# An empty step ahead of a head's first value products, and the last product of a convolution copied out of its PSUM bank

## The chip, the core and the metric

The kernel runs on one core of a Trainium2 chip. The core has TensorE (matrix products, PE in the profile, its weight loads PEld), VectorE (DVE), ScalarE (ACT), GpSimd (POOL) and SyncE (SP, here a queue that issues transfers). They run side by side and wait for each other through semaphores. Products are written into PSUM, eight banks of 128 x 512 floats, and are read out of it by VectorE and ScalarE; everything else lies in SBUF. The metric is the device time of one execution in microseconds (us), as the median of the runs.

## The reference, cut to what matters

Two layers of one mixer, over 1024 positions and 1024 columns, with eight heads of 256 in each layer: four mLSTM heads, whose q and k go through a short causal convolution and a SiLU, and four retention heads, whose q and k are rotated.

```python
for l in range(DEPTH):
    h = rmsnorm(x, norm_g[l]) * (1.0 + scale) + shift
    p = h @ w_in[l]
    mq, mk, mv, mo, mz, mi, mf, rq, rk, rv, rz = split_cols(p)
    qk = jax.nn.silu(causal_dwconv(jnp.concatenate([mq, mk], -1), conv_w[l], conv_b[l]))
    cell = mlstm_chunkwise(...)        # four heads
    y_m = sigmoid(mo) * head_layernorm(cell, gn_m[l]) * silu(mz)
    ret = retention_chunkwise(...)     # four heads
    y_r = head_layernorm(ret, gn_r[l]) * silu(rz)
    x = x + gate * (jnp.concatenate([y_m, y_r], -1) @ w_out[l])
return rmsnorm(x, final_g)
# within a head, for each chunk of positions:
#   s = (q k^T) * decay;  o = s v + (q C) * decay;  C = decay * C + k^T v
```

## The kernel before

**Products.** Every operand is split into a high part and a rest, and each product is three matmuls (`mm3`, lines 181 to 183). The projections of a layer run as a list of jobs. A job takes two blocks of 128 columns (q, k, or a gate) and builds them out of seven products of 12 matmuls, in the manner of Strassen: a11, S1, S2, a12, S4, S3, a22. A job for values (`v`) takes two heads, and each of its seven products comes in two parts of 24 smaller matmuls. One such product or part is called a slot here; there are 238 of them in a layer. The weights of a slot are loaded by SP some seven slots ahead, their high part is made by ScalarE (L408) and the rest by VectorE (L413).

**Banks.** The products of a q or k job gather in three banks: one called X, used by a11, S2, S3 and a22, one called Y and one called Z. Y and Z share a pair of buffers (`pz`), X has a pair of its own (`px`), which the jobs take in turn. A value job takes both buffers of each pair: its third slot (a11, part 0) starts in one `px` buffer and its fourth (a11, part 1) in the other, which the job ahead of it used for its own X.

**Convolution.** `pair_product` hands each finished quarter to `done`. For q and k of the mLSTM heads that launches `conv_chain`: one scaled copy by ScalarE (L889), three shifted multiply-adds by VectorE (L894), a tanh (L897) and a last multiply (L899). For the quarter of the last product, a22, the chain reads its input straight from the X bank, so the bank is free when the third multiply-add has read it. Before that, `halo` (L767) copies the last three columns of the bank.

**Attention of a head.** It runs between the slots. After each slot the kernel ticks, and the head whose turn it is does the next step of `TABLE` (L985). A step is a list of short words. `S0` to `S3` are the scores of a chunk: a product q k^T (L1045), scaled by VectorE (L1061 to L1064), then split into `sH` by ScalarE (L1083) and `sL` by GpSimd (L1084). `V001` are the first value products of a head, for both halves of chunk 0: nine matmuls on L1126, six that read `sH` and three that read `sL`. `V10` to `V31` are the later ones, which also multiply q with the state, split into `cH` and `cL` (L1135, then three matmuls with `sH` and `sL`). `U01` to `U5` update the state from k, whose split parts are the tiles `b` (L933, L934). `q`, `k`, `v`, `t`, `d` issue loads on SP; `Q`, `K`, `s`, `m` split or prepare what was loaded.

**One head at a time.** A head can start four ticks after its k job has ended, but only when `busy` is false. The head ahead of it clears that flag at step `RELEASE` (22). The table has 31 steps, numbered from 0.

The order on TensorE is the order in which the code is written. On the other engines the order is set by the framework's scheduler, which places an instruction by priority and by its own estimate of when its inputs are there.

Of the kernel before, what the change touches and what calls it, by code (L numbers as in the profile page):

```python
# [37 lines left out]
NACC = 12  # L38
# [49 lines left out]
def tile_hybrid_trunk(ctx, tc, x, xt, c, positions, w_ada, b_ada, norm_g, w_in, w_blk, w_val, conv_w, conv_b,  # L88
                      b_igate, b_fgate, gn_m, gn_r, w_out, final_g, consts, out):
    nc = tc.nc  # L90
    V, A, G, PE, Q = nc.vector, nc.scalar, nc.gpsimd, nc.tensor, nc.sync
# [13 lines left out]
    def nm(s):  # L105
        uid[0] += 1
        return f"{s}_{uid[0]}"
# [6 lines left out]
    def wt(tag, n, bufs, dt=F32):  # L114
        t = wrk.tile([P, 516 if tag == "acc" else n], dt, tag=tag, bufs=bufs, name=nm(tag))
        if tag == "acc" and not apart:
            apart.append(wrk.tile([P, 32], F32, tag="apart", bufs=1, name="apart"))
        return t[:, 0:n] if tag == "acc" else t
# [4 lines left out]
    def ps_x():  # L123
        return pp.tile([P, 512], F32, tag="x", bufs=2, name=nm("px"))

    def ps_z():
        return pp.tile([P, 512], F32, tag="z", bufs=2, name=nm("pz"))
# [25 lines left out]
    def launch(gen, delay=0, last=0):  # L153
        uid[0] += 1
        pending.append([clock[0] + delay, uid[0] + last * 1000000, gen])
# [24 lines left out]
    def mm3(o, lt, rt, start, stop, more=False):  # L180
        PE.matmul(o, lt[0], rt[0], start=start, stop=False, skip_group_check=more)  # L181
        PE.matmul(o, lt[0], rt[1], start=False, stop=False, skip_group_check=more)  # L182
        PE.matmul(o, lt[1], rt[0], start=False, stop=stop, skip_group_check=more)  # L183
# [575 lines left out]
                                                    for r, h in got for a in range(2)] for n in at})  # L759
        return add  # L760

    def pair_product(F, done, loose=False, conv=False):
        bank, keep, full = {}, {}, {}

        def halo(n, pt):
            if conv:
                V.tensor_copy(full[n][:, 0:3], pt[:, HALF - 3:HALF])  # L767

        def product(n, part, w):
            b, form = PRODUCT[n]  # L770
            new = b not in bank
            if new:
                bank[b] = ps_x() if b == "X" else ps_z()
            for k in range(4):
                mm3(bank[b], w[k], F[form][k], new and k == 0, k == 3, b != "Y")
            with tc.high_priority():
                if n in ("a11", "S1", "S2"):
                    full[n] = wt("acc", 515, NACC)
                    keep[n] = full[n][:, 3:515]
                    A.copy(keep[n], bank[b])  # L780
                elif n == "a12":
                    c = keep["a11"] if loose else bank["Y"]
                    V.tensor_tensor(c, bank["Y"], keep["a11"], ALU.add)
                    halo("S2", c)
                    done(0, 0, c)
                elif n == "S3":
                    V.tensor_tensor(keep["S1"], bank["X"], keep["S1"], ALU.add)
                    done(1, 1, full["S1"] if conv else keep["S1"])
                elif n == "S4":
                    V.tensor_tensor(keep["S2"], bank["Z"], keep["S2"], ALU.add)  # L790
                    done(0, 1, full["S2"] if conv else keep["S2"])
                else:
                    halo("S1", bank["X"])
                    done(1, 0, bank["X"])
        return product

    def vpair_product(l, F, heads):
# [65 lines left out]
    def z_done(store):  # L863
        def done(m, half, src):
            launch(z_gate(src, wt("acc", 512, NACC), -1.0 if m else 1.0, store[m][half]))
        return done

    def zo_done(store):
        g, got = {}, {}

        def done(o, half, src):
            got[o, half] = src
            if not o:
                g[half] = wt("acc", 512, NACC)
                launch(z_gate(src, g[half], 1.0))
            if (1 - o, half) in got:
                launch(o_gate(got[1, half], g[half], store[half], -1.0, 1 - o))
        return done
# [63 lines left out]
    def conv_done(l, hg, which):  # L942
        late_one = []

        def one(m, half, src, delay=0):
            launch(conv_chain(l, hg, which, m, half, src), delay)

        def done(m, half, src):
            if m and half:
                late_one.append(src)  # L950
                return
            one(m, half, src)
            if m:
                one(1, 1, late_one[0], 1)
        return done
# [20 lines left out]
    def load_rotary(rot):  # L976
        for which in range(2):
            for i in range(2):
# [3 lines left out]
                rot[which].append(t[:, 0:HALF])  # L982

    busy = [False]
    TABLE = ("q0 k0 d0 t0", "", "v0", "Q0 K0 m0 d1", "s0 k1", "S0", "m1 q1 K1", "v1", "Q1", "V001 t1", "S1 k2 q2", "U01",  # L985
             "s1 d2 K2", "v2 Q2", "V10 U2 m2", "S2", "t2 d3", "V11 U3 k3", "s2 q3", "v3 K3", "Q3 m3", "V20 U4",
             "S3", "", "V21 U5", "", "", "", "V30", "V31", "")
    RELEASE = 22

    def attention(l, hg, gt):  # L990
        h, ml = hg % 4, hg < 4
# [245 lines left out]
        busy[0] = True  # L1237
        for n, step in enumerate(TABLE):
            if n == RELEASE:
                busy[0] = False  # L1240
# [234 lines left out]
    for l in range(DEPTH):  # L1475
# [23 lines left out]
        if l == 0:  # L1499
# [10 lines left out]
            for step in script.split():  # L1510
                what, arg = step[0], [int(d) for d in step[1:]]
# [3 lines left out]
                if what in "SQ":  # L1515
                    half, tt, cc = arg
                    o, xi, acc = wt("acc", 512, NACC), xts[half][tt][cc], xss[half][:, tt, cc:cc + 1]
# [75 lines left out]
        F = {}  # L1593
# [13 lines left out]
        jobs = [(w[0], [int(d) for d in w[1:]]) for w in plan.split()]  # L1607
# [14 lines left out]
        feed = Feeder(-1, [job_forms(j) for j in jobs], slots)  # L1622
        launch(adaptive(l, gcol, gb), 40 if l else 30)

        def job_product(what, arg):
            h = arg[0]
            if what == "v":
                return vpair_product(l, F, arg)
            if what == "z":
                return pair_product(F, z_done(gdr[l][h]))  # L1630
            if what == "a":
                return pair_product(F, zo_done(gdr[l][h][arg[1]]))
            which = int(what == "k")
            if h == 4 and not which:
                load_rotary(rot)
            if h > 3:
                return pair_product(F, rot_done(l, h, which, *rot), True)
            return pair_product(F, conv_done(l, h, which), conv=True)

        going, forms, left = {}, {}, {}  # L1640
        loads = OutLoads(l)
# [1 line left out]
            left[j] = left.get(j, 0) + 1  # L1643
        for j, n, part in slots:
            if j not in going:
                going[j] = job_product(*jobs[j])
            feed.step()
            if part == 0:
                forms[j] = feed.take(j, n)
            going[j](n, part, forms[j])  # L1650
            tick()
            if sum(left.values()) == 5:
                loads.fetch(2)
            elif sum(left.values()) == 3:
                loads.make()
            left[j] -= 1
            if left[j] == 0 and jobs[j][0] == "k":
                launch(attention(l, jobs[j][1][0], gt), 4, 1)
# [11 lines left out]
        for half in range(2):  # L1670
# [15 lines left out]
            else:  # L1686
                ready = []
                launch(residual_later(1, 1, ready))
                last = row_evac(gb, xn, ss, lambda tt: final_scale(xn, roots[tt], tt, 1, fg), ready)
# [36 lines left out]
```

## Time and profile before

| what | value |
|---|---|
| median of 3 runs | 2192.43 us (2189.73 to 2194.45) |
| the profiled execution | 2190.59 us, of which the span of the program's instructions is 2188.9 us |
| TensorE busy | 2105.7 us, 96% of the span |
| VectorE busy | 1775.1 us, 81% |
| ScalarE busy | 1149.3 us, 53% |
| GpSimd busy | 671.1 us, 31% |
| mean granted TensorE clock | 0.989 of full speed |

A busy TensorE is not one at its peak: a matmul's record lasts from its start to its modelled end, and the records overlap. In rows of the profile `px<-b,wH 128*128 128x512` reads: into a tile `px` from tiles `b` and `wH`, a 128 by 128 weight, 128 x 512 results. A wait is put down to the instruction whose semaphore came last.

### The profile page before, as it was taken

The numbers are of one execution on the slowest core, as the hardware profiler recorded it, in microseconds if no ns is written. First come the engines' busy times: TensorE is split into PE (matmuls) and PEld (weight loads), VectorE is DVE, ScalarE is ACT, GpSimd is POOL, SyncE is SP. The second block draws the span as 40 slices with busy tenths as digits, with TensorE's granted clock in tenths as the row PEclk, the third lists the DMA queues.
The fourth block names the chain that finished last, engine by engine and source line by source line (L and its number), as shares of the span: only waits on it lengthen the run. The fifth ranks groups of instructions, "written<-read, shape, count | busy, mean of one in ns | idle before, by whom it ended". The sixth has DMA issues, their size and how long they took to land.

```text
span 2188.9 us, 34934 instructions
## 1 busy us (share of the span) xinstructions
PE 2105.7 (96%) x11489; PEld 1818.2 (83%) x11489; DVE 1775.1 (81%) x3287; ACT 1149.3 (53%) x2151; POOL 671.1 (31%) x616
## 2 busy tenths in 40 slices
PE   7899999999999999999999999999999999999998
PEld 5698889887988778888887889788988887888887
DVE  6897897999889898874639688898898888978563
ACT  7545335345565656653545434444556565665343
POOL 1421123233232333324565113322323332231313
PEclk9999999999999999999999999999999999999999
DMA  8268779788787767786633777977876676687874
GB/s 292 60 202 236 219 220 269 205 225 235 195 236 191 188 179 215 195 273 230 209 108 93 188 196 210 252 204 215 230 196 193 187 220 189 185 205 248 228 252 119
DMA packets 451971, 448.43 MB, mean 205 GB/s; under 512 B 191218, under 2 KB 308410, under 8 KB 451788
## 3 DMA queue, kind: packets, MB, share of 16 engines
q1 hardware_dynamic: 432060, 410.27, 61.3%
q0 software_dynamic: 19584, 35.66, 10.7%
q8 instruction: 90, 1.47, 0.3%
q14 instruction: 93, 0.76, 0.1%
q10 hardware_dynamic: 144, 0.26, 0.0%
HBM read 322.76 MB, written 123.31 MB: 204 GB/s over the span
## 4 chain that ended last, share of the span: by engine, by line
PE 47%; DVE 11%; DMA 5%; issue 3%; ACT 1%; POOL 1%; SPq 1%; DVEq 0%; POOLq 0%; ACTq 0%
PE px L181 6%; PE px L182 6%; PE px L183 6%; PE pz L181 5%; PE pz L182 5%; PE pz L183 4%; PE pa L183 4%; PE pa L181 3%; PE pa L182 3%; DVE R L413 2%; DVE acc L894 2%; PE pa L1135 1%; DMA acc<-kfr 1%; PE pa L1045 1%; DVE R L718 1%
## 5 line engine op out<-in xcount | busy, mean ns | idle before, releaser
L408 ACT CAST wH<-R 128x512 fp32r<-128x512 f32 x616 | 378.9, 618 | 494.4 <-PE px L182 161.0
L413 DVE TENSOR_TENSOR R<-R,wH 128x512 fp32r<-128x512 f32 x544 | 404.2, 748 | 123.4 <-ACT wH L408 121.1
L181 PE MATMUL px<-b,wH 128*128 128x512 f32 x912 | 359.9, 395 | 3.5 <-ACT acc L780 2.7
L182 PE MATMUL px<-b,wH 128*128 128x512 f32 x912 | 358.6, 393 | 0.0
L183 PE MATMUL px<-b,R 128*128 128x512 f32 x912 | 358.0, 393 | 0.0
L182 PE MATMUL pz<-b,wH 128*128 128x512 f32 x704 | 275.3, 391 | 1.6 <-DVE b L1271 1.6
L181 PE MATMUL pz<-b,wH 128*128 128x512 f32 x704 | 276.5, 393 | 0.0
L183 PE MATMUL pz<-b,R 128*128 128x512 f32 x704 | 275.0, 391 | 0.0
L714 POOL DMA_DIRECT2D R<-in_w_blk_dram x104 | 92.6, 890 | 379.1 <-DMA R<-in_w_blk_dram 191.1
L181 PEld LDWEIGHTS px<-b,wH 128*128 128x128 f32 x912 | 172.9, 190 | 39.1 <-ACT acc L780 3.9
L183 PEld LDWEIGHTS px<-b,R 128*128 128x128 f32 x912 | 172.9, 190 | 37.3
L182 PEld LDWEIGHTS px<-b,wH 128*128 128x128 f32 x912 | 172.8, 189 | 32.9
L181 PE MATMUL px<-wH,b 128*128 128x256 f32 (+1 forms) x576 | 173.2, 301 | 13.8 <-DVE acc L894 5.0
L182 PE MATMUL px<-R,b 128*128 128x256 f32 (+1 forms) x576 | 172.4, 299 | 8.3 <-DVE R L413 8.3
L183 PE MATMUL px<-wH,b 128*128 128x256 f32 (+1 forms) x576 | 171.9, 298 | 0.0
L183 PEld LDWEIGHTS pz<-b,R 128*128 128x128 f32 x704 | 132.5, 188 | 28.4
L182 PEld LDWEIGHTS pz<-b,wH 128*128 128x128 f32 x704 | 132.8, 189 | 27.5 <-DVE b L1271 2.4
L181 PEld LDWEIGHTS pz<-b,wH 128*128 128x128 f32 x704 | 132.8, 189 | 25.9 <-ACT acc L780 0.4
L882 POOL TENSOR_TENSOR kc<-acc,kc 128x512 fp32r<-128x512 f32 x64 | 91.7, 1434 | 193.3 <-ACT kc L881 169.3
L413 POOL TENSOR_TENSOR R<-R,wH 128x512 fp32r<-128x512 f32 x72 | 96.6, 1344 | 164.8 <-ACT wH L408 145.8
L882 POOL TENSOR_TENSOR q<-acc,q 128x512 fp32r<-128x512 f32 x64 | 93.5, 1461 | 131.8 <-ACT q L881 123.5
L181 PE MATMUL pz<-wH,b 128*128 128x256 f32 (+1 forms) x448 | 133.8, 299 | 0.0
(348 smaller groups left out, 5203.9 us busy)
## 6 DMA issues: line engine op xcount, KB each, us to landing
R<-in_w_blk_dram SPq DMA_DIRECT2D x276, 256.0 KB
vdr<-acc SPq DMA_DIRECT2D x128, 256.0 KB
ring<-vdr SPq DMA_DIRECT2D x64, 512.0 KB
R<-in_w_out_dram SPq DMA_DIRECT2D x128, 256.0 KB
R<-in_w_blk_dram POOLq DMA_DIRECT2D x104, 256.0 KB, 4.7
R<-in_w_val_dram SPq DMA_DIRECT2D x80, 256.0 KB
gdr<-acc SPq DMA_DIRECT2D x64, 256.0 KB
acc<-in_w_ada_dram SPq DMA_DIRECT2D x64, 256.0 KB
```

Source lines behind the costliest of these rows:

```text
L181: PE.matmul(o, lt[0], rt[0], start=start, stop=False, skip_group_check=more)
L182: PE.matmul(o, lt[0], rt[1], start=False, stop=False, skip_group_check=more)
L183: PE.matmul(o, lt[1], rt[0], start=False, stop=stop, skip_group_check=more)
L408: A.copy(h, r)
L413: eng.tensor_tensor(lo, r, f(h), ALU.subtract)
L714: G.dma_start(raw[n], src, accum_op=ALU.add)
L718: V.tensor_tensor(raw[n], raw[one], raw[two], ALU.add)
L882: eng.tensor_tensor(dst[1], src, f(dst[0]), ALU.subtract)
L894: V.scalar_tensor_tensor(acc[:, e:], pt[:, o + e - d:o + HALF - d], wcol, acc[:, e:], ALU.mult, ALU.add)
L1045: PE.matmul(pd, piece(kx[j], i, dt, tt * P, P), qd, start=dt == 0 and i == 0, stop=dt == 1 and i == 1)
L1135: PE.matmul(pi[:, 0:W], piece(qs[j], i, dt, tt * P, P), state[part][:, dt, 0:W], start=part + dt + i == 0, stop=ml and part + dt == 2)
```

## The change

Two edits. First, `TABLE` gets an empty step in front of "V001 t1", and one of the three empty steps behind "V21 U5" goes. So V001 and all steps from there to V21 come one slot later after a head's start, V30 and V31 stand where they stood, and the table keeps its 31 steps. `RELEASE` goes from 22 to 23, which is the step "S3" in both tables; the next head can start one slot later. Second, where the job behind a convolution job is a value job, `pair_product` copies the X bank of a22 into an SBUF tile by ScalarE, and the chain reads that tile. In the job lists this is so for k of head 0 in layer 0 and for k of head 1 in layer 1. (k of two retention heads also stands ahead of a value job; they don't get the copy.)

```diff
-    def pair_product(F, done, loose=False, conv=False):
+    def pair_product(F, done, loose=False, conv=False, free=False):
...
                 else:
                     halo("S1", bank["X"])
-                    done(1, 0, bank["X"])
+                    last = bank["X"]
+                    if free:
+                        last = wt("acc", 512, NACC)
+                        A.copy(last, bank["X"])
+                    done(1, 0, last)
...
-    TABLE = ("q0 k0 d0 t0", "", "v0", "Q0 K0 m0 d1", "s0 k1", "S0", "m1 q1 K1", "v1", "Q1", "V001 t1", "S1 k2 q2", "U01",
+    TABLE = ("q0 k0 d0 t0", "", "v0", "Q0 K0 m0 d1", "s0 k1", "S0", "m1 q1 K1", "v1", "Q1", "", "V001 t1", "S1 k2 q2", "U01",
              "s1 d2 K2", "v2 Q2", "V10 U2 m2", "S2", "t2 d3", "V11 U3 k3", "s2 q3", "v3 K3", "Q3 m3", "V20 U4",
-             "S3", "", "V21 U5", "", "", "", "V30", "V31", "")
-    RELEASE = 22
+             "S3", "", "V21 U5", "", "", "V30", "V31", "")
+    RELEASE = 23
...
-        def job_product(what, arg):
+        def job_product(what, arg, free=False):
...
-            return pair_product(F, conv_done(l, h, which), conv=True)
+            return pair_product(F, conv_done(l, h, which), conv=True, free=free)
...
-                going[j] = job_product(*jobs[j])
+                going[j] = job_product(*jobs[j], j + 1 < len(jobs) and jobs[j + 1][0] == "v")
```

Line numbers from 795 on are four higher in the changed kernel (L1126 is L1130, L1135 is L1139, L894 is L898).

Three places show what moves. The first is TensorE in layer 0, from the scores of chunk 0 of head 7 (`pa<-q,kc`) to its V001 (`pa<-ring,sH`); of each slot between them stands the first matmul. Before:

```order
L1045 MATMUL pa_6393<-q_6316,kc_6319 128x256 x4
L181 MATMUL px_6153<-b_1099,wH_6279 128x512
...
L181 MATMUL px_6453<-b_630,wH_6327 128x512
...
L181 MATMUL pz_6501<-b_1094,wH_6367 128x512
...
L181 MATMUL px_6153<-b_1438,wH_6405 128x512
...
L1126 MATMUL pa_6556<-ring_353,sH_6491 128x256 x2
```

And of the change:

```order
L1049 MATMUL pa_6429<-q_6343,kc_6346 128x256 x4
L181 MATMUL px_6445<-b_630,wH_6310 128x512
...
L181 MATMUL pz_6492<-b_1094,wH_6354 128x512
...
L181 MATMUL px_6129<-b_1438,wH_6391 128x512
...
L181 MATMUL px_6445<-b_1090,wH_6443 128x512
...
L181 MATMUL pz_6585<-b_860,wH_6488 128x512
...
L1130 MATMUL pa_6604<-ring_353,sH_6522 128x256 x2
```

Between scores and V001 there were four slots, and there are five. The scores themselves stand one slot later (the slot that reads `b_1099` came behind them and now comes ahead), since this head waits for the head ahead of it; so V001 stands two slots later among the products.

The second place is VectorE in layer 1, where the X bank of k of head 1 is read (`px_19489` before, `px_19449` after). Before, its reads are the halo copy and three multiply-adds:

```order
L767 COPY acc_19538<-px_19489 128x3
...
L894 SCALAR_TENSOR_TENSOR acc_19799<-px_19489,cols_1153,acc_19799 128x511
...
L894 SCALAR_TENSOR_TENSOR acc_19799<-px_19489,cols_1153,acc_19799 128x510
...
L413 TENSOR_TENSOR R_20064<-R_19730,wH_20062 128x512
L899 SCALAR_TENSOR_TENSOR acc_19755<-acc_19870,acc_19755 128x512
L894 SCALAR_TENSOR_TENSOR acc_19799<-px_19489,cols_1153,acc_19799 128x509
```

And of the change, on VectorE the halo copy, then the multiply-adds, which read the tile `acc_19763`:

```order
L767 COPY acc_19491<-px_19449 128x3
...
L898 SCALAR_TENSOR_TENSOR acc_19765<-acc_19763,cols_1153,acc_19765 128x511
...
L898 SCALAR_TENSOR_TENSOR acc_19765<-acc_19763,cols_1153,acc_19765 128x510
...
L898 SCALAR_TENSOR_TENSOR acc_19765<-acc_19763,cols_1153,acc_19765 128x509
```

On ScalarE the copy stands here, among the rows that scale a normalised chunk (L1194) and the convolution's first step (L893):

```order
L901 ACTIVATE acc_19739<-acc_19626 128x512
L1194 ACTIVATE nd_19499<-nd_19499,nmu_19741,rsd_19694 128x256
L797 COPY acc_19763<-px_19449 128x512
L1194 ACTIVATE nd_19499<-nd_19499,nmu_19741,rsd_19694 128x256
L408 CAST wH_19915<-R_19664 128x512
L893 ACTIVATE acc_19765<-acc_19763,cols_1153 128x512
```

VectorE's last read of the bank was its third multiply-add, 24 rows behind the halo copy; it is now the halo copy, and ScalarE's is the copy.

The third place is TensorE in layer 1, from the last state update of head 4 (`pa<-ring,b`) to its V30 (`pa<-cH,q`); of each slot stands the first matmul. Before:

```order
L183 MATMUL pa_15912<-ring_353,b_15613 128x256
L181 MATMUL px_15846<-b_13374,wH_15779 128x512
...
L181 MATMUL pz_15968<-b_12830,wH_15842 128x512
...
L181 MATMUL pz_15877<-b_13209,wH_15874 128x512
...
L1045 MATMUL pa_16021<-q_15957,kc_15960 128x256 x4
L181 MATMUL px_15846<-b_13383,wH_15924 128x512
...
L1135 MATMUL pa_16057<-cH_15905,q_15709 128x256 x4
```

And of the change:

```order
L183 MATMUL pa_15939<-ring_353,b_15654 128x256
L181 MATMUL pz_15953<-b_12832,wH_15818 128x512
...
L181 MATMUL pz_15875<-b_13211,wH_15872 128x512
...
L181 MATMUL px_15822<-b_13385,wH_15898 128x512
...
L1139 MATMUL pa_16047<-cH_15932,q_15751 128x256 x4
...
L1049 MATMUL pa_16058<-q_15977,kc_15980 128x256 x4
```

Four slots and the scores of the next head stood between the update and V30; now three slots do, and the next head's scores come behind V30.

## The prediction

> **What bounds the kernel now.** I read the page first, then TensorE's list of waits, then the windows and timelines around the waits that this change can reach.
>
> ```profile
> span 2188.9 us, 34934 instructions
> PE 2105.7 (96%) x11489; PEld 1818.2 (83%) x11489; DVE 1775.1 (81%) x3287; ACT 1149.3 (53%) x2151; POOL 671.1 (31%) x616
> ```
>
> TensorE sets the time: it is idle for only 2188.9 - 2105.7 = 83 us. A change that leaves the matmuls as they are can win only from these 83 us and from stretches at a low clock. TensorE's waits, longest in total first (who waited, for whom, us in total, times, longest):
>
> ```profile
> PE px L182 <- DVE R L413: 8.3, 3, 5.6
> PE px L1556 <- DMA b<-in_w_ada_dram: 8.2, 1, 8.2
> PE pa L1126 <- ACT sH L1083: 8.2, 4, 4.1
> PE pa L1126 <- POOL sL L1084: 6.3, 7, 2.9
> PE pa L183 <- DVE b L934: 5.4, 6, 1.7
> PE px L181 <- DVE acc L894: 5.0, 1, 5.0
> ```
>
> Two of these entries are the places of the change. L1126 is V001, the first value products of a head, waiting for the split scores: 8.2 + 6.3 = 14.5 us in 11 waits, spread over 7 of the 16 heads. The last row is one wait of 5.0 us for the multiply-adds of a convolution, the X bank of k of head 1 in layer 1. The three that cost most at V001:
>
> ```profile
> 544.74 1.16 PE L1126 MATMUL pa<-ring,sH 128*128 128x256 f32 x6 [4.08 <-ACT sH L1083]
> 546.50 0.58 PE L1126 MATMUL pa<-ring,sL 128*128 128x256 f32 x1 [0.61 <-POOL sL L1084]
> 721.10 1.00 PE L1126 MATMUL pa<-ring,sH 128*128 128x258 f32 x6 [0.69 <-ACT sH L1083]
> 724.99 0.63 PE L1126 MATMUL pa<-ring,sL 128*128 128x258 f32 x3 [2.89 <-POOL sL L1084]
> 1407.07 0.98 PE L1126 MATMUL pa<-ring,sH 128*128 128x256 f32 x6 [2.97 <-ACT sH L1083]
> 1408.93 0.58 PE L1126 MATMUL pa<-ring,sL 128*128 128x256 f32 x1 [0.88 <-POOL sL L1084]
> ```
>
> They are 4.69 us (head 7, layer 0), 3.58 us (head 1, layer 0) and 3.85 us (head 5, layer 1). A wait costs more than its idle time. In the windows below (length, then busy time of PE, PEld, DVE, ACT and POOL, then the granted clock) the clock is at half right behind the three waits and behind the bank's wait, and it is 1.00 or near it around them:
>
> ```profile
> 545.37:552.19 6.82, 6.21 (x18) 4.85 (x18) 4.21 (x11) 1.84 (x4) 2.95 (x4) 0.50 0.92 274
> 726.27:729.68 3.41, 3.41 (x10) 2.64 (x9) 0.88 (x7) 0.02 (x1) 0.73 (x2) 0.50 0.91 197
> 1408.94:1412.35 3.41, 3.41 (x10) 2.83 (x11) 3.41 (x8) 1.09 (x2) 1.63 (x2) 0.50 0.81 252
> 1719.55:1722.96 3.41, 2.85 (x13) 2.85 (x14) 3.41 (x10) 2.15 (x4) 1.70 (x3) 0.50 0.11 29
> ```
>
> TensorE works 6.21 + 3.41 + 3.41 + 2.85 = 15.9 us there at half speed, so about 7.9 us are lost.
>
> **The change, part by part.** No matmul and no VectorE operation is added or dropped; two ScalarE copies are added. What matters is how far things move, and the unit is a slot:
>
> ```profile
> 244.40:266.14 21.74, 21.74 (x97) 18.01 (x96) 20.29 (x34) 8.65 (x15) 1.73 (x2) 1.00 0.73 199
> ```
>
> Eight slots of 12 matmuls, without attention work between them, take 21.74 us: 2.72 us a slot.
>
> *V001.* The scores' chain (scaling, `sH`, `sL`) gets five slots in place of four. That is one slot, 2.72 us, for a head that starts when it did. A head that waits for the head ahead also starts later, because `RELEASE` is one higher. Counting ticks, head 7 in layer 0 and head 5 in layer 1 start one slot later, so their V001 stands two slots (5.4 us) later among the products; head 1 in layer 0 starts as before. What is late there is VectorE's backlog of product work, which stands at the same products as before:
>
> ```profile
> 500.00:540.65 40.65, 40.65 (x213) 34.67 (x211) 40.33 (x73) 24.21 (x46) 13.30 (x12) 1.00 0.77 224
> 540.65:547.40 6.75, 2.06 (x11) 1.76 (x11) 6.75 (x12) 2.50 (x6) 3.10 (x2) 0.85 0.96 272
> 547.40:556.00 8.60, 8.60 (x33) 7.04 (x33) 2.87 (x10) 3.81 (x9) 4.04 (x5) 0.72 0.92 248
> ```
>
> For 40 us ahead of head 7's wait VectorE has no gap (40.33 of 40.65). So two slots cover 4.69 and 3.85 us, and one covers all but 3.58 - 2.72 = 0.9 us of head 1's. The four smaller waits, 14.5 - 12.1 = 2.4 us together, are covered. Gain: 14.5 - 0.9 = 13.6 us of idle time, and the half-speed stretches go with it: 7.9 us with the bank's.
>
> *The bank.* The rows tell why TensorE waited 5.0 us:
>
> ```profile
> 1706.98 0.15 DVE L767 COPY acc<-px 128x3 f32<-128x3 f32 x1
> 1707.70 0.76 ACT L889 ACTIVATE acc<-px,cols 128x512 f32<-128x512 f32 x1
> 1710.45 0.74 DVE L894 SCALAR_TENSOR_TENSOR acc<-px,cols,acc 128x511 f32<-128x511 f32 x1
> 1714.90 0.73 DVE L894 SCALAR_TENSOR_TENSOR acc<-px,cols,acc 128x510 f32<-128x510 f32 x1
> 1719.33 0.73 DVE L894 SCALAR_TENSOR_TENSOR acc<-px,cols,acc 128x509 f32<-128x509 f32 x1
> 1720.11 0.58 PE L181 MATMUL px<-wH,b 128*128 128x256 f32 x1 [5.04 <-DVE acc L894]
> ```
>
> The bank is read first at 1707 and last at 1719.33, because three multiply-adds of 0.74 us stand among 24 rows of VectorE. Afterwards the halo copy and ScalarE's copy are the last readers. They stand where the first readers stand now, near 1708, and TensorE wants the bank at 1715.1 (1720.11 - 5.04). The whole wait goes: 5.0 us. The copy's price is that of the same copy for other banks, and the multiply-adds cost the same from either source:
>
> ```profile
> L780 ACT COPY acc<-px 128x512 f32<-128x512 f32 x104 | 60.3, 580 | 8.8 <-PE px L183 5.0 <-DMA kfr<-acc 2.4 <-DMA vdr<-acc 1.4
> L894 DVE SCALAR_TENSOR_TENSOR acc<-acc,cols,acc x96: 704/740/3739, 511.2 to 1901.7; 128x512 f32<-128x512 f32 x96
> L894 DVE SCALAR_TENSOR_TENSOR acc<-px,cols,acc x48: 699/737/749, 522.4 to 1900.6; 128x511 f32<-128x511 f32 x16, 128x510 f32<-128x510 f32 x16, 128x509 f32<-128x509 f32 x16
> ```
>
> Two copies are 1.2 us of ScalarE, which is 53% busy; behind them queue a normalising scale, a weight cast and the chain itself, none of which TensorE waits for in that stretch. I take 0, with 1.2 us if that cover is gone. In layer 0 the same edit removes no wait, since TensorE has none for L894 there (the row above counts one in all).
>
> *V30.* It now follows the last state update by three slots in place of four, and where heads follow closely the next head's scores no longer stand between. So the fourth chunk's inputs lose 2.72 us of lead, or about 4 us with the scores (six matmuls took 0.98 us in a row above, so ten take some 1.4). The two tightest leads are those of `sL`, in layer 1 at head 4 and head 1 (GpSimd's row, then TensorE's row that reads it):
>
> ```profile
> 1391.45 1.29 POOL L1084 TENSOR_TENSOR sL<-acc,sH 128x384 fp32r<-128x384 f32 x1
> 1394.21 0.28 PE L183 MATMUL pa<-ring,sL 128*128 128x256 f32 x1
> 1816.54 1.27 POOL L1084 TENSOR_TENSOR sL<-acc,sH 128x384 fp32r<-128x384 f32 x1
> 1819.99 0.28 PE L183 MATMUL pa<-ring,sL 128*128 128x258 f32 x1
> ```
>
> The leads are 1394.21 - 1392.74 = 1.5 and 1819.99 - 1817.81 = 2.2 us, so new waits of 4.0 - 1.5 = 2.5 and 2.7 - 2.2 = 0.5 us. With about 1 us for heads near the edge I charge 4 us. The bounds are 0, if the scheduler pulls the scores forward, and 43.5 us, a whole slot in all 16 heads.
>
> *The backlog.* VectorE catches up while TensorE stands still. Take the stand away and it may be late at the next product that needs it, which is `PE pa L183 <- DVE b L934` (state updates, 5.4 us already) or a bank that it empties. At head 7 VectorE is idle for 8.60 - 2.87 = 5.7 us right behind, and V001 has moved two slots: nothing is charged. Behind 1408.94 it is full (3.41 of 3.41), so I charge half of 3.85 + 1.7, or 2.8 us. Behind the bank's wait it is full until 1725 and then has 7.3 us free:
>
> ```profile
> 1704.00:1725.00 21.00, 15.96 (x120) 15.49 (x119) 21.00 (x45) 8.25 (x15) 3.11 (x4) 0.92 0.36 98
> 1725.00:1745.00 20.00, 20.00 (x169) 20.00 (x169) 12.73 (x28) 13.33 (x27) 5.25 (x5) 1.00 0.88 282
> ```
>
> I charge a third of 6.4 us, 2.2. Together 5 us. The bounds are 0 and the whole gain at V001, about 20 us.
>
> *Later heads and their loads.* Heads that wait start one to three slots later, and with them their loads of q, k, v, decay rows and turned k on SP, past some of the weight loads. TensorE's three waits for weights (L413, 8.3 us above) lie ahead of each layer's first head, the first and the last of them here:
>
> ```profile
> 106.52 0.58 PE L182 MATMUL px<-R,b 128*128 128x256 f32 x1 [5.61 <-DVE R L413]
> 1186.83 0.39 PE L182 MATMUL px<-R,b 128*128 128x256 f32 x1 [0.41 <-DVE R L413]
> ```
>
> So weights are late nowhere in the heads' stretch, and the last head's outputs are wanted only some 14 products into the output stage. I take 0, and as the bound 5 us either way, the size of the state updates' entry above.
>
> **The sum.** -13.6 (V001) - 7.9 (half speed) - 5.0 (bank) + 4 (V30) + 5 (backlog) = -17.5 us. The profiled execution took 2190.6 us (its span and 1.7 us around it), which makes 2173.1; the median of the runs is 1.8 us above it, so I say 2175 us. The likeliest case alone runs from 2166 to 2183.
>
> The Trainium skill's page "TensorE: Matmul & The Clock Gate", section "HAM oscillation — how this bites in real kernels", puts the return to half clock behind idle gaps of more than about 3.4 us. The trace differs: 2.97 and 0.88 us with six matmuls between were enough at 1407. By that rule only the stretches at 545 and 1719 hang on these waits, the term would be 4.5 us in place of 7.9, and the sum would come out at 2178; I follow the trace.
>
> **Rivals.**
>
> 1. *Half the gain at V001.* If the backlog moves along with a head's scores, a later start buys nothing and every head gains one slot only. Then 4.69 - 2.72 = 2.0, 1.1 and 0.9 us stay, 3.1 more than charged, and two half-speed stretches with them, (6.21 + 3.41) / 2 = 4.8. That is 2175 + 7.9 = 2183. For it: VectorE's 40 full us. Against: its product work keeps its place. Chance 0.14.
> 2. *The backlog comes back whole.* VectorE, not the order, is the bound in those stretches, and all of V001's gain returns as waits for `b` or for banks. Only the bank's 5.0 + 1.4 stays, less 4 at V30: 2192.4 - 2.4 = 2190, which is no change. Against: 5.7 us idle behind 547. Chance 0.13.
> 3. *Slower.* V30 and V31 become the wait in every head. Gross gain without that term is 21.5 us, so it decides from 21.5 / 16 = 1.35 us a head; at 2 us a head the time is 2192.4 - 21.5 + 32 = 2203. For it: the lead of 1.5 us shown. Against: the next tightest is 2.2, so few heads reach it. Chance 0.11.
> 4. *The copy doesn't free the bank early.* It stands behind a normalising scale that waits for GpSimd's root and for VectorE; if that is late, ScalarE holds the bank as VectorE did. That takes 6.4 back: 2181. Against: 7 us of room. Chance 0.04.
>
> **Chances and range.** The forecast has 0.58. A measurement of this kernel tells a change from none at about 0.2%, 4.4 us. Faster by more than that are the forecast, rivals 1 and 4 and a sixth or so of rival 2: 0.78. Within it, the rest of rival 2: 0.11. Slower: 0.11. The range reaches down to the gross gain with a little more, 2192.4 - 28 = 2164, and up to rival 2: 2190.
>
> **What would show each step.** V001's waits (L1130 in the changed kernel) fall from 14.5 us to under 2. The wait of `px L181` for the multiply-add (L898) is gone, and a copy of 0.58 us on L797 ends near the first reads. No half-speed stretch remains at those four places. `pa L183` waits for `sL` grow by some 4 us at V30. If `pa L183 <- DVE b` (L938) grows by 10 us or more, rival 2 is right; if V001 keeps about 4 us, rival 1; if V30's waits stand in most heads, rival 3. The forecast is wrong if TensorE's idle time falls by less than 8 us, or if new waits stand where none is charged, at the scores' `kc` and `q` or at a value job's banks.

## The result, and the profile after

The changed kernel took 2215.55 us (median of 4 runs, 2214.00 to 2219.22), the kernel before 2191.08 us beside it (4 runs). The ratio is 1.0115, 95% interval 1.0101 to 1.0129: slower by some 24 us, where 17 us less were forecast. Lines from L795 on stand four higher in the changed kernel (L1126 is L1130, L1084 is L1088).

The head of its page:

```profile
span 2212.4 us, 34989 instructions
PE 2111.7 (95%) x11489; PEld 1823.3 (82%) x11489; DVE 1788.2 (81%) x3287; ACT 1147.1 (52%) x2153; POOL 678.1 (31%) x616
```

Of the 23.5 us by which the span grew, TensorE's idle time (span less busy) is 17.5 us: 83.2 before, 100.7 after. The other 6.0 us are longer busy time with the same 11489 matmuls. VectorE has the same 3287 instructions and is busy 13.1 us longer. TensorE's waits after:

```profile
PE pa L183 <- POOL sL L1088: 15.7, 7, 4.0
PE pa L183 <- DVE b L938: 11.3, 10, 1.9
PE px L181 <- ACT acc L780: 7.1, 3, 3.3
PE px L181 <- DVE acc L968: 6.3, 2, 3.9
PE pa L181 <- ACT sH L1087: 3.4, 2, 1.7
PE pz L181 <- DVE acc L790: 2.7, 2, 1.6
PE pa L1130 <- POOL sL L1088: 2.3, 3, 1.5
```

V001 (L1130) fell from 14.5 to 2.3 us and the convolution's bank is gone from the list, both as forecast. What is new stands in the first two rows: L183 is the last of the three matmuls of a split product, and it waits for `sL` of the next scores, S1, and for `b` of the state update. I sorted the gaps ahead of TensorE's matmuls by the step they belong to (told by their tiles and their order in a head). In us, for both kernels:

| | S0 | V001, U01 | V10, U2 | V20, U4 | V30 | px and pz | all gaps |
|---|---|---|---|---|---|---|---|
| before | 6.3 | 17.0 | 1.3 | 4.8 | 0.0 | 38.0 | 75.2 |
| after | 1.9 | 2.3 | **25.4** | 6.5 | 0.1 | 46.6 | 92.7 |

So V001 and U01 gave back 14.7 us, and V10 with U2, the next attention products behind them, took 24.1. 11.8 of the 25.4 us stand in the three heads whose V001 had waited 12.1 us before (head 7 and head 1 of layer 0, head 5 of layer 1).

The distance from S1 to V10 is four steps in both tables; what changed is when S1's results are there. For head 1 of layer 0, the rows are S1's product, its `sL`, and V10's matmul that reads it. Before:

```profile
729.78 1.11 PE L1045 MATMUL pa<-q,kc 128*128 128x256 f32 x8
740.91 0.74 POOL L1084 TENSOR_TENSOR sL<-acc,sH 128x256 fp32r<-128x256 f32 x1
744.08 0.28 PE L183 MATMUL pa<-ring,sL 128*128 128x258 f32 x1
```

And after:

```profile
739.83 1.13 PE L1049 MATMUL pa<-q,kc 128*128 128x256 f32 x8
757.30 1.01 POOL L1088 TENSOR_TENSOR sL<-acc,sH 128x256 fp32r<-128x256 f32 x1
758.36 0.58 PE L183 MATMUL pa<-ring,sL 128*128 128x258 f32 x1 [4.04 <-POOL sL L1088]
```

From the end of S1's product to the end of `sL` it was 10.8 us and is now 17.4. Head 7 of layer 0 went from 9.2 to 17.1 us, head 5 of layer 1 from 8.7 to 15.7, and the mean of all 16 heads from 9.8 to 13.1. Of these 3.4 us, 2.5 lie ahead of `sH` (VectorE's scaling and ScalarE's turn) and 0.7 between `sH` and the start of `sL` (GpSimd's queue).

Some of those waits, and what stood ahead of one of them, head 6 of layer 1 at 1534 us (timeline of the changed kernel: start, length, engine, line, idle time before and what ended it):

```profile
576.17 0.38 PE L183 MATMUL pa<-ring,sL 128*128 128x256 f32 x1 [2.57 <-POOL sL L1088]
578.39 0.58 PE L183 MATMUL pa<-ring,b 128*128 128x256 f32 x1 [1.47 <-DVE b L938]
758.36 0.58 PE L183 MATMUL pa<-ring,sL 128*128 128x258 f32 x1 [4.04 <-POOL sL L1088]
...
1525.01 0.86 DVE L1077 SCALAR_TENSOR_TENSOR acc<-pa,kc,rmask 128x256 f32<-128x256 f32 x2
1525.80 0.68 DVE L413 TENSOR_TENSOR R<-R,wH 128x512 fp32r<-128x512 f32 x1
1526.39 0.68 DVE L1113 TENSOR_TENSOR cL<-cf,cH 128x512 fp32r<-128x512 f32 x1
1527.00 0.70 DVE L1201 STREAM_TRANSPOSE zt<-nd 128x512 f32<-128x512 f32 x1
1527.20 1.30 POOL L886 TENSOR_TENSOR q<-acc,q 128x512 fp32r<-128x512 f32 x1
1527.63 1.43 DVE L970 TENSOR_TENSOR acc<-acc,acc 128x512 f32<-128x512 f32 x1
1528.98 0.68 DVE L413 TENSOR_TENSOR R<-R,wH 128x512 fp32r<-128x512 f32 x1
1529.58 0.41 DVE L1079 TENSOR_TENSOR acc<-acc 128x256 f32<-128x256 f32 x1
1530.48 0.39 PE L181 MATMUL pa<-ring,sH 128*128 128x256 f32 x1 [1.72 <-ACT sH L1087]
1532.33 1.00 POOL L1038 TENSOR_SCALAR_AFFINE_SELECT dm<-dm 128x128 f32<-128x128 f32 x2 [3.83 <-DMA dm<-mdr]
1533.31 1.14 POOL L1088 TENSOR_TENSOR sL<-acc,sH 128x256 fp32r<-128x256 f32 x1
1534.51 0.58 PE L183 MATMUL pa<-ring,sL 128*128 128x256 f32 x1 [3.52 <-POOL sL L1088]
```

S1's scores are scaled on VectorE at 1525.01, and the addition that completes them (L1079) comes 4.57 us later, because five other VectorE instructions stand between them. One of these, L970, takes 1.43 us in place of some 0.7, while GpSimd's split of q (1.30 us) runs. ScalarE makes `sH` at once, and TensorE has waited 1.72 us for it. Then `sL` stands in GpSimd's queue behind a select that waits for its transfer until 1532.33, which costs 3.52 us more. In three more of V10's waits for `sL` (2.57 us at 576, 4.04 at 758 and 1.75 at 1902), `sL` started 1.9 to 4.3 us after `sH` was ready, behind GpSimd's splits, load issues, or selects that waited. That is lateness of engines that work in order, met by whichever product asks next.

The clock: nothing at half speed is left at V001 and at the bank, but there are new stretches at 576, 1447 and 1904 (V10 and U2), 757 and 1532 (V10) and 788 (U4). Two of them, in windows (length, busy time of PE, PEld, DVE, ACT, POOL, then the granted clock):

```profile
758.40:761.80 3.40, 3.40 (x12) 3.01 (x13) 3.40 (x8) 0.62 (x1) 0.00 (x0) 0.50 0.77 162
1447.20:1450.40 3.20, 3.20 (x10) 2.52 (x9) 3.20 (x8) 0.39 (x1) 0.00 (x0) 0.51 0.74 191
```

Between 500 and 1910 us the kernel before has eight stretches at half speed, in which TensorE works 29.3 us, and the changed one has eleven, with 43.0 us. 13.7 us more at half speed cost some 6.8 us (an estimate, half of 13.7), and the busy time grew by 6.0. So the longer busy time can be put down to the clock.

### The profile page after: what moved, and what is told of

Same layout as the page of the kernel before. It is cut to its first block, busy times and chain, and to the rows that moved or that the text cites. A ratio compares the mean times of both kernels' runs of the same rounds, so it can differ in the third digit from the quotient of the medians.

```text
span 2212.4 us, 34989 instructions
## 1 busy us (share of the span) xinstructions
PE 2111.7 (95%) x11489; PEld 1823.3 (82%) x11489; DVE 1788.2 (81%) x3287; ACT 1147.1 (52%) x2153; POOL 678.1 (31%) x616
## 5 line engine op out<-in xcount | busy, mean ns | idle before, releaser
L413 DVE TENSOR_TENSOR R<-R,wH 128x512 fp32r<-128x512 f32 x544 | 414.4, 767 | 121.2 <-ACT wH L408 115.8
L183 PE MATMUL px<-b,R 128*128 128x512 f32 x912 | 357.8, 392 | 0.0
L183 PE MATMUL pz<-b,R 128*128 128x512 f32 x704 | 276.4, 393 | 0.0
L183 PEld LDWEIGHTS px<-b,R 128*128 128x128 f32 x912 | 172.4, 189 | 37.2
L183 PE MATMUL px<-wH,b 128*128 128x256 f32 (+1 forms) x576 | 172.6, 300 | 0.0
L183 PEld LDWEIGHTS pz<-b,R 128*128 128x128 f32 x704 | 133.4, 189 | 28.5
L886 POOL TENSOR_TENSOR kc<-acc,kc 128x512 fp32r<-128x512 f32 x64 | 92.6, 1447 | 206.1 <-ACT kc L885 187.3
```

Of the source, the lines that this page charges most:

```text
L413: eng.tensor_tensor(lo, r, f(h), ALU.subtract)
L886: eng.tensor_tensor(dst[1], src, f(dst[0]), ALU.subtract)
```

## The experiments

Each run is compared with the kernel before on the same chip; the interval is 95%. Expectations are quoted as they were written before the runs.

**The parts of the change.** Copy alone:

```diff
 # old TABLE, RELEASE = 22
+    if free:
+        last = wt("acc", 512, NACC)
+        A.copy(last, bank["X"])
```

> The old table and release, with only the copy of the a22 bank on ScalarE in the two convolution jobs that value products follow. Theory A (the late inputs of V10 come with the empty step and the later starts): the copy does what the sum said, the waits of px L181 on L894 (5.0 us in the profile before) go, nothing else changes: 2186 us (2181 to 2190). Theory B (the copy itself does the harm: one more instruction in ScalarE's order and one acc tile held, so that px waits on acc of L780 and L968, which rose from 2.7 and 2.1 to 7.1 and 6.3 us): 2197 to 2205 us, with those waits as high as in the changed kernel.

Measured: 2192.21 us, ratio 0.9994 (0.9978 to 1.0010). No harm, but no 5 us either; the waits that theory B names (L780 and L968) are 3.7 and 1.3 us, not 7.1 and 6.3. The copy reads the bank by 1702.3, and the product that had waited 5.04 us (a11, part 1, of the value job) starts without a wait at 1709.19. The wait stands one slot later, 24 matmuls on, under another name (timeline of this run):

```profile
1701.69 0.57 ACT L797 COPY acc<-px 128x512 f32<-128x512 f32 x1
1709.19 0.28 PE L181 MATMUL px<-wH,b 128*128 128x256 f32 x1
...
1717.21 0.63 ACT L901 ACTIVATE acc<-acc 128x512 f32<-128x512 f32 x1 [1.99 <-DVE acc L898]
1717.74 0.57 ACT L834 COPY acc<-px 128x512 f32<-128x512 f32 x1
...
1718.37 0.58 PE L181 MATMUL px<-wH,b 128*128 128x256 f32 x1 [6.14 <-ACT acc L834]
```

This next product (S2, part 0) goes on in the other X bank of the value job, which ScalarE's copy L834 must have read first. That copy stands behind the tanh L901, which waits for VectorE's late multiply-add (L898). The wait of 5.04 us became one of 6.14 for the same VectorE work, one product later and through ScalarE's queue. In the changed kernel the two next slots (S2, parts 0 and 1) wait 0.99 and 1.46 us for L834.

Table and release without the copy, then each by itself:

```diff
 # e2_table: new TABLE, RELEASE = 23, no copy
 # e3_step22: new TABLE, RELEASE = 22, no copy
 # e4_rel23: old TABLE, RELEASE = 23, no copy
```

> The new table and release without the copy. Theory A (table and release cost what was lost): 2215.6 + 5 = 2220 us (2214 to 2226), V10's banks wait 20 us or more for sL, sH and U2's b as in the changed kernel, and the 5.0 us of px L181 on L894 are back. Theory B (the copy does the harm): 2180 to 2195 us.

> The new table with the old RELEASE of 22, without the copy: the empty step alone, heads start in the steps in which they started before. Theory A1 (the empty step takes away V001's waits, in which VectorE and GpSimd caught up with their queues, so that S1's sL and U2's b come late at V10 and V11 instead): the loss stays, 2205 to 2225 us, V10's gaps 15 us or more. Theory A2 (the later head starts do the harm, since each head then stands beside other product jobs): the forecast's gain shows, 2172 to 2185 us, V10's gaps under 6 us.

> The old table with RELEASE 23, without the copy: only the head starts move, by one to three steps. Theory A1 (the empty step does the harm): 2185 to 2197 us, V001's wait for sL stays near 14 us and V10's gaps small. Theory A2 (the starts do the harm): 2205 to 2230 us, with V10's gaps 15 us or more.

Measured: table and release 2212.62 us, 1.0078 (1.0054 to 1.0102); the empty step alone 2201.62, 1.0033 (1.0018 to 1.0048); the release alone 2204.56, 1.0045 (1.0030 to 1.0060). In the second of these the next head's v0 is loaded into the buffer that V21 and U5 still read, so these multiply other values; no work is dropped by it. So each half alone makes the kernel slower, and the two add up (0.33% and 0.45% against 0.78%). A1 and A2 were put as alternatives; the empty step alone falls between their ranges (V10 and U2 14.2 us), the release alone at the lower edge of A2's, so both causes are real. With the release alone V001's gaps fall to 8.0 us though the table is the old one, and V10 and U2 have 15.0: moving the head by a slot against the product work is enough to move the wait.

The empty step and the copy once more, with the heads starting as before and every value intact:

```diff
-    TABLE = ("q0 k0 d0 t0", "", "v0", "Q0 K0 m0 d1", ...
-    RELEASE = 23
+    TABLE = ("q0 k0 d0 t0", "", "", "v0 Q0 K0 m0 d1", ...
+    RELEASE = 22
```

> The changed kernel with RELEASE 22 and the load of v0 one step later in its head (so that it does not overtake V21 U5 of the head before): empty step and copy as in the change, heads start where they started in the kernel before. If the later starts cost half of the loss (the run with RELEASE 23 alone lost 10 us), 2200 to 2207 us, V10 and U2 about 13 us (V001's 14.5 us come back there, in the heads L0 k7, k1 and L1 k5). If the empty step costs it all, 2211 to 2220 us. If the forecast was right for the step alone, 2175 to 2185 us.

Measured: 2201.52 us, 1.0044 (1.0025 to 1.0062). The first expectation holds in its time and in its 12.6 us at V10 and U2, but not in the heads: of the three that it names, head 7 of layer 0 has no such wait, head 1 0.3 us and head 5 of layer 1 4.2; the other 8.1 us stand in five heads that had waited little or not at all at V001. The gaps (us):

| | S0 | V001, U01 | V10, U2 | V20, U4 | V30 | px and pz | all gaps |
|---|---|---|---|---|---|---|---|
| before | 6.3 | 17.0 | 1.3 | 4.8 | 0.0 | 38.0 | 75.2 |
| step and copy, old starts | 2.0 | 2.1 | 12.6 | 13.3 | 1.5 | 40.4 | 79.6 |
| release alone | 3.3 | 8.0 | 15.0 | 10.2 | 0.2 | 41.7 | 84.7 |

S0, V001 and U01 gave back 19.1 us, V10 to V30 took 21.4. The entry that grew most, in this kernel's list of waits, is VectorE's work for the state update, 5.4 us before:

```profile
PE pa L183 <- DVE b L938: 22.2, 10, 5.1
```

**More distance at V10 too.** An empty step before V10, two sparse steps behind it merged:

```diff
-    "V10 U2 m2", "S2", "t2 d3", "V11 U3 k3", "s2 q3",
+    "", "V10 U2 m2", "S2 t2 d3", "k3", "V11 U3 s2 q3",
```

> The changed kernel with V10 U2, S2 t2 and V11 U3 one step later against S1 (an empty step before V10, the two empty-handed steps behind merged), V20 and all that follows where it was. Theory D (distance: S1's sL and U2's b merely need one slot more, as V001 did): the waits of V10 and U2, 25 us in the changed kernel, fall under 8 us and do not turn up again, 2195 to 2205 us. Theory L (VectorE and GpSimd are behind by then, and whoever asks first waits for them): the waits come back at V11, U3, V20 and U4, PE's idle total stays at 85 us or more, 2208 to 2225 us.

Measured: 2198.27 us, 1.0021 (1.0001 to 1.0040), 17 us less than the change. V10 and U2 fall to 3.6 us; V20, now one step nearer to S2, has 7.2 and V30 5.0. Distance does help, and part of the lateness turns up at later products. Theory D is right in the time and at V10 and U2; theory L is right that the waits don't all go: TensorE's idle time is 90.0 us, where L had 85 or more.

**Which engine is late.** Each replacement was made in both kernels. Transposes of the normalised values as copies on ScalarE:

```diff
-    late(V.transpose(z.rearrange("p (b t c) -> p t b c", ...), nrm[j]...))
+    late(A.copy(z.rearrange("p (a b) -> p a b", a=2), nrm[j]))
```

> The kernel before with the 64 transposes of the normalised values (L1197, 700 ns each, 44.8 us of VectorE) replaced by plain copies on ScalarE; it leaves out the transposition. Theory L with VectorE as the engine that is behind: V001's 14.5 us and the other waits for VectorE's results shrink by half, 2172 to 2184 us. Theory G (GpSimd's own queue is behind: K2 and Q2 splits, selects on dm, load issues stand ahead of sL): V001's waits for sL stay over 10 us, 2186 to 2194 us.

> The changed kernel with the same replacement (transposes of the normalised values as plain copies on ScalarE; the transposition is left out). Theory L with VectorE behind: it gains more than the kernel before does, since its new waits at V10, U2 and U4 (29 us) hang on VectorE: 2180 to 2198 us, V10 and U2 under 12 us together. Theory G: V10's waits for sL stay at 12 us or more, 2206 to 2216 us.

The subtraction that makes `sL` on VectorE:

```diff
-    G.tensor_tensor(lo, src, f(hi), ALU.subtract)
+    V.tensor_tensor(lo, src, f(hi), ALU.subtract)
```

> The kernel before with sL (L1084) subtracted on VectorE instead of GpSimd. Theory G (sL is late for GpSimd's queue, its 1.07 us and the hold it lays on VectorE): V001's 14.5 us fall to 5 or less, 2178 to 2187 us. Theory L (VectorE is behind and gets 64 instructions of some 0.4 us more, 26 us): 2190 to 2205 us, V001 waits for sL on VectorE instead.

> The changed kernel with sL subtracted on VectorE. Theory G: V10's waits for sL (15.7 us with V20's) fall under 5 us, 2190 to 2203 us. Theory L: they stay over 10 us, now on VectorE, 2212 to 2228 us.

The subtraction of the K and Q splits: first as a copy on ScalarE, then as a copy on GpSimd, then on VectorE:

```diff
-    split_to((t[:, 0:512], t[:, 512:1024]), raw)
+    A.copy(t[:, 0:512], raw); A.copy(t[:, 512:1024], raw)           # e8, e9
+    A.copy(t[:, 0:512], raw); G.tensor_copy(t[:, 512:1024], raw)    # e13, e14
+    split_to((t[:, 0:512], t[:, 512:1024]), raw, V)                 # e15, e16
```

> The changed kernel with the 128 subtractions of the K and Q splits (L886 on GpSimd, 1.4 us each, some 185 us of its time) replaced by a second copy on ScalarE; the low parts of K and Q are left out. Theory G (GpSimd's queue, and VectorE held up while GpSimd's two-operand instructions run: nmu 128x2 takes up to 1.27 us then, 0.15 us otherwise): V10's waits for sL fall under 4 us, VectorE's busy time falls from 1788 to 1765 us or less, 2178 to 2196 us. Theory L with VectorE alone behind: VectorE's time stays within 8 us of 1788, the waits for b and acc stay, 2204 to 2216 us.

> The kernel before with the 128 subtractions of the K and Q splits on GpSimd replaced by a second copy on ScalarE, as in the run of the changed kernel that took 2177 us; the low parts of K and Q are left out. If GpSimd's two-operand work is what turned the change into a loss, the two kernels come out level without it: 2170 to 2182 us. If it only slows both alike (VectorE held up), and the loss has another cause, the kernel before keeps its lead of some 20 us: 2150 to 2165 us.

> The changed kernel with the subtraction of the K and Q splits (L886, GpSimd, two operands) replaced by a one-operand copy on GpSimd: GpSimd keeps 128 instructions there, the low parts are wrong by that. Theory H (VectorE is held while GpSimd's two-operand instructions run, and that hold makes its results late): VectorE's busy time falls by 50 us or more, 2172 to 2190 us. Theory Q (what made sL and b late is the place that these instructions take in GpSimd's queue): 2205 to 2216 us.

> The kernel before with the same replacement by a one-operand copy on GpSimd. Theory H: 2172 to 2182 us, within 8 us of the changed kernel with it. Theory Q: 2185 to 2194 us, 15 us or more ahead of it.

> The kernel before with the subtraction of the K and Q splits on VectorE (complete, nothing left out). Under theory H VectorE gets 128 instructions of some 0.7 us, 90 us, and is rid of some 75 us of holds: 2185 to 2198 us, level with the kernel before. Under theory Q VectorE only gets more: 2200 to 2225 us.

> The changed kernel with the subtraction of the K and Q splits on VectorE (complete). Theory H: 2188 to 2203 us, nearer to the kernel before than the change is. Theory Q: 2220 to 2250 us.

Measured (us; ratios to the kernel before; in each cell the old table, then the change; gaps as above):

| replaced | time | ratio | VectorE busy | V001, U01 | V10, U2 |
|---|---|---|---|---|---|
| nothing | 2191.1, 2215.6 | 1, 1.0115 | 1775, 1788 | 17.0, 2.3 | 1.3, 25.4 |
| transposes | 2183.7, 2202.0 | 0.9963 (0.9944 to 0.9983), 1.0047 (1.0026 to 1.0069) | 1734, 1749 | 7.5, 0.4 | 6.1, 18.1 |
| sL to VectorE | 2193.6, 2203.5 | 1.0004 (0.9988 to 1.0020), 1.0057 (1.0036 to 1.0078) | 1778, 1788 | 10.9, 1.5 | 5.5, 23.3 |
| splits, ScalarE copy | 2176.8, 2177.2 | 0.9935 (0.9917 to 0.9953), 0.9934 (0.9913 to 0.9956) | 1704, 1708 | 8.0, 0.0 | 1.7, 12.1 |
| splits, GpSimd copy | 2170.4, 2171.6 | 0.9902 (0.9885 to 0.9919), 0.9927 (0.9898 to 0.9956) | 1718, 1721 | 10.2, 1.1 | 3.2, 11.8 |
| splits on VectorE | 2213.1, 2196.8 | 1.0106 (1.0087 to 1.0125), 1.0025 (1.0014 to 1.0036) | 1774, 1779 | 19.9, 0.2 | 10.7, 18.9 |

What follows:

- In all six rows the old table waits most at V001, the new one at V10 and U2. In the first five the two columns together don't fall by more than 0.5 us from the old table to the new: the empty step moves the wait. In the last they fall, from 30.6 to 19.1.
- GpSimd's own queue isn't needed for the wait, though it has a share in it. With `sL` taken from it the change is 12 us faster, but V10 and U2 still have 23.3 us, and the same two entries now both name VectorE:

```profile
PE pa L183 <- DVE b L938: 15.3, 11, 3.7
PE pa L183 <- DVE sL L1088: 12.4, 7, 2.7
```

- The loss shrinks as VectorE's load does. Where VectorE is lighter by 57 to 80 us (the two copies in place of the splits) the tables are level, 0.4 and 1.2 us apart. With some 40 us less (transposes) both gain, the change 13.5 and the kernel before 7.4 us, and 18 us stay between them. That VectorE's load alone makes the tables level is not shown, since the copies took work from GpSimd too (678 us busy in the change, 488 and 585 with them).
- The two copies don't tell hold from queue. The GpSimd copy takes 0.8 us where the subtraction took 1.5, and it doesn't wait for ScalarE's high part, so queue and hold shrank together. The expectation's word "two operands" was wrong (see the last section).
- The last row turned the order round: with the splits on VectorE the old table is the slower one by 16 us, with VectorE about as busy as ever. So the price of a table is not a property of the table; it depends on how its steps fall against VectorE's product work. Theory Q's range holds for the kernel before and theory H's for the change, so neither holds for both. Why just this placement suits the new table was not settled.
- The other expectations: in the rows of the transposes and of `sL` the kernel before is in theory L's range, and the changed kernel ends between the ranges of its two theories (2202.0 and 2203.5 us), in the second with its waits as theory L had them. The times with a copy for the splits lie in the ranges of theory G, of "level" and of theory H, or up to 2 us below them.

**Both cures.** V10 one step later, with the splits, or with `sL`, on VectorE; nothing is left out:

> The changed kernel with V10 U2 one step later (as in the run of 2198 us) and the subtraction of the K and Q splits on VectorE (as in the run of 2197 us), complete. If the two cures add up (17 us and 18 us of the change's 2215.6), 2178 to 2186 us, faster than both kernels. If they mend the same waits (VectorE's lateness at V10 and U2), 2192 to 2200 us. If VectorE is late wherever the table puts the next consumer, 2200 to 2215 us.

> The changed kernel with V10 U2 one step later and sL on VectorE (as in the run of 2203.5 us), complete. If the two add up (17 and 12 us), 2183 to 2191 us. If they mend the same waits, 2192 to 2200 us; if VectorE is late wherever the next consumer stands, 2200 to 2215 us.

Measured: with the splits 2185.28 us, 0.9972 (0.9957 to 0.9987); with `sL` 2183.31 us, 0.9960 (0.9943 to 0.9976). Both are in the range for cures that add up: the second is 9 us faster than the kernel before beside it (2192.21 us) and 32 us faster than the change. What is left of the lateness in the second now stands at V20 and V30, 12.4 us, and V10 and U2 have 1.5. The head of its page, and the two entries of its list of waits that grew with it (the state's low part, and `sL`):

```profile
span 2187.1 us, 34921 instructions
PE 2105.7 (96%) x11489; PEld 1821.9 (83%) x11489; DVE 1780.5 (81%) x3351; ACT 1151.3 (53%) x2153; POOL 615.1 (28%) x552
```

```profile
PE pa L1139 <- DVE cL L1113: 5.0, 5, 2.3
PE pa L183 <- DVE sL L1088: 4.8, 4, 2.4
```

## Why the prediction was wrong

**V001** was right: charged at -13.6 us, measured 14.5 to 2.3, -12.2. The remainder was expected at head 1 of layer 0 and is mostly at head 7 (1.49 us). S0 and U01 lost another 6.9 us of waits that the sum didn't have, which was luck.

**The backlog** is the step that failed. It was charged with 5 us, because VectorE had free time behind head 7's wait and V001's own wait was taken as the place where lateness costs. The runs showed 24.1 us more at V10 and U2 (4.0 of it at head 7, where nothing was charged), and 9 us more at `px` and `pz`. Two things were missed. First, while TensorE stood at V001, VectorE and GpSimd worked off what lay ahead of S1's scores, and S1 and V10 follow V001 at a fixed distance. The idle time was a lead for the next scores: without it S1's chain ends 3.4 us later in the mean, and 6.6 to 7.9 us later in the three heads with the long waits, where 11.8 us came back for 12.1. I looked for the return at the products next to the wait, in the old timeline, and not at S1 to V10, where the wait itself had given the lead. Which heads pay depends on their starts too: with the old starts these three have 4.5 us at V10 and U2. Second, the bound "the whole gain at V001" was not one: with the heads' starts as before, 19.1 us left at S0, V001 and U01, and 21.4 came back.

**Later heads** were charged at 0, within 5 us either way, by looking at weight loads alone. The release alone costs 0.45%, some 10 us: the heads' products meet VectorE's product work at another place (V10 and U2 15.0 us). Weight loads are not the cause: TensorE's wait for them is 8.3 us as before. Other loads have a part: in the longest V10 wait of that run, 3.01 us at 655, `sL` stands behind two selects of GpSimd that had waited for their transfers.

**Half speed** was charged at -7.9 us. The four stretches are gone, but eight in all became eleven, so the term is some +6.8 us (the estimate above) in place of -7.9.

**The bank**: -5.0 us was charged. The copy does free the bank early, as the prediction said and rival 4 doubted, and the product that had waited starts at once. But the sum took the end of this wait for a gain and didn't look at the next product, which needs the same VectorE work through ScalarE: with the copy alone it waits 6.14 us. It is the backlog's mistake once more. In the changed kernel 2.45 us are left at the two next slots, where without the copy (table and release alone) the old place waits 3.98. The copy on top of the table shows no gain (1.0115 against 1.0078, intervals that barely touch); that was not followed up.

**V30** was charged at +4 us and as rival 3 at far more: it has 0.1 us. **Rival 2** had the mechanism, VectorE as the bound and V001's gain returning as waits for `b` and for banks, at a chance of 0.13. Its sign, 10 us more of `pa L183 <- DVE b`, didn't come (5.4 to 11.3 us); the larger part came as waits of V10 for `sL`, 13.0 us, which the prediction looked for at V30 alone. Its time of 2190 was too low by 25 us, since it held the return to be at most the gain and the starts to be free.

## What to carry to other kernels

An idle stretch of the busiest engine is also the lead of everything behind it. Before pushing a waiting step back, look at the next step that needs the same late engines and stands at a fixed distance behind the moved one, and ask what its lead is without the stretch. Move both, or shorten the late engines' work: here the pair of steps and 64 subtractions moved together gave 9 us, the pair of steps with the subtractions where they were still lost 0.2%, and the one step alone lost more.

## What the runs showed of the hardware

VectorE's busy time in a profile holds time in which it stands still. An instruction of 128 x 2 elements takes 0.15 us, but far more when GpSimd runs beside it, and then the two end together (timeline of the changed kernel, first GpSimd, then VectorE):

```profile
1470.46 1.72 POOL L886 TENSOR_TENSOR q<-acc,q 128x512 fp32r<-128x512 f32 x1 [0.26 <-ACT q L885]
1470.93 1.27 DVE L1192 SCALAR_TENSOR_TENSOR nmu<-mv,rsd 128x2 f32<-128x2 f32 x1
```

They end at 1472.18 and 1472.20. The mean of that group rose with the change; the groups of the kernel before and of the changed one:

```profile
L1188 DVE SCALAR_TENSOR_TENSOR nmu<-mv,rsd 128x2 f32<-128x2 f32 x64 | 12.4, 194 | 14.6 <-POOL rsd L1185 14.5
```

```profile
L1192 DVE SCALAR_TENSOR_TENSOR nmu<-mv,rsd 128x2 f32<-128x2 f32 x64 | 20.4, 318 | 13.0 <-POOL rsd L1189 13.0
```

I expected this of GpSimd's two-operand instructions. A one-operand copy does it too (timeline of the changed kernel with the GpSimd copy):

```profile
841.98 0.76 POOL L1017 CAST q<-acc 128x512 fp32r<-128x512 f32 x1 [0.93 <-DMA acc<-qdr]
842.20 0.56 DVE L1182 SCALAR_TENSOR_TENSOR va<-qd 128x2 f32<-128x2 f32 x1
```

The Trainium skill's page "SBUF — State Buffer", section "Who interferes with whom", says that a VectorE instruction with two SBUF inputs contends with a GpSimd instruction that reads SBUF, and that the ports they share are an exclusive lock; these rows agree. In this kernel 128 splits of 1.4 to 1.5 us on GpSimd were worth 57 to 80 us of VectorE's busy time, when a shorter copy on GpSimd or none at all stood in their place.
